# Output projection opened inside the attention of a two-layer streaming trunk: six tiles over the finished heads as fill, and the last memory head from PSUM into the projection's operand

## The chip, the cores and the metric

The kernel runs on one core of one Trainium2 chip. The metric is the device time of one execution in microseconds (us); the comparison uses the median of several runs. A profile of one execution gives the times of single instructions.

## The reference

The reference runs a two-layer encoder trunk over 1056 tokens, 1024 of a new stream and 32 of a running one, with a width of 1024. What matters here, for one layer:

```python
h = rmsnorm(x) @ w_in                       # 1024 wide: token mixer | 4 memory query heads
a = pool_mix(h[:, :512])                    # layer 0; differential attention in layer 1
k, v = split(rmsnorm(mem) @ w_mem)          # 256 memory tokens, 4 heads of 128
m = softmax(q @ k.T * 128 ** -0.5) @ v      # memory attention; the 32 sample tokens use cached k, v
x = x + concat(a, m) @ w_out                # output projection, 1024 x 1024
x = x + relu(rmsnorm(x) @ w1) ** 2 @ w2     # 4096 wide
```

The outputs are `x` after a last norm, the memory keys and values, and pooling and key/value caches.

## The kernel before

Activations lie transposed, features on the 128 partitions: 8 chunks `c` of 128 features. The 1056 tokens are three groups `g` of 352 columns (`GW`). All products are made in full fp32 precision from two parts: a high part (a cast by ScalarE) and a low part (a subtraction on VectorE or on GpSimd, which the profile calls POOL), see `split`. A product is three matmuls (`mm3`): high by high, low by high, high by low. So in the trace lines L49, L50 and L51 are all matmuls of that kind, L54 and L55 the split.

A program run has four stages: start and mixing of layer 0 (`mix0`), output projection and feed-forward of layer 0 (`tail(0)`), mixing of layer 1 (`mix1`), `tail(1)`. Each stage has its own PSUM pool (`ps0` to `ps3`).

In the mixing stages a driver (`drive`, `step`) runs the steps of the attention units (a head's scores, its softmax, and later its transposes and values) and takes steps of a generator `fill0` or `fill1` between them, so that TensorE has other products to do while a softmax runs. The memory attention goes over four heads of two halves of 512 tokens; the 32 sample tokens of all four heads are one further unit, `mem_sample`. `mem_values` transposes the probabilities (L391), splits them (`aTh`, `aTl`), multiplies by the values, copies the result from PSUM (`mo`) and stores it to the DRAM scratch `oscr[l][4 + h]`; the token mixer's heads go to `oscr[l][0..3]`.

`tail(l)` loads the 24 tiles `o` (one for each group and chunk, 176 KB) from `oscr`, splits them into `xh[g]`, `xl[g]` (`take`; for chunks 1, 3 and 5 POOL makes the low part), and loads `x`. `project` then multiplies by `w_out`, a row of weights `W[j]` for each output chunk `j`. Before any other tile it opens six (`g` 0 and 1 by `j` 0 to 2) over chunks 0 to 6, in PSUM banks `xb` and `dn`, and closes them with chunk 7, the last memory head.

Weights stream from DRAM through a ring of six buffers `wraw` (256 KB each, `NRAW`), and `part` casts and subtracts them into `whi`, `wlo` (eight buffers each, `NW`); `weights` lists their order and the engine that subtracts. All these loads, and all stores, are issued by one queue, SP, in program order; an issue that must wait holds those behind it. Within an engine the order of the instructions is set by a scheduler when the program is built, from the order in the code; the engine then takes them strictly in that order. Tile names in the listings below carry a number; `pr` are probabilities, `st` softmax sums, `mk` and `mv` the memory keys and values in parts, `mkr` and `mvr` as loaded, `mks` and `mvs` as just projected, `ms` the sample's, `dh` and `dl` the parts of the pooled difference, `S` its running sums.

Of the kernel before, what the change touches and what calls it, by code (L numbers as in the profile page):

```python
# [17 lines left out]
NS = 32  # L18
# [22 lines left out]
class Kern:  # L41
# [15 lines left out]
    def weights(self):  # L57

        t, v, g = self.t, self.nc.vector, self.nc.gpsimd
        for k in (0, 1, 2, 3):  # L60
            yield t["w_in"][k], None, v
        for j in range(8):
            yield t["w_mem"][j], None, v
        yield t["w_in"][4], None, g
        yield t["w_in"][5], None, g
        for j in range(4):
            yield t["w_mem"][8 + j], None, v
        yield t["w_in"][6], None, g
        yield t["w_in"][7], None, g
        for j in range(4, 8):  # L70
            yield t["w_mem"][8 + j], None, v
        for l in range(2):
            if l:
                for h in range(4):
                    yield t["w_kv"][h], GKV, g
                    yield t["w_kv"][4 + h], GKV, g
                    yield t["w_in"][8 + h], GA + 8, g
                for h in range(4):
                    yield t["w_in"][12 + h], GA + 8, g
            for j in (*range(8), 0, 1, 2):  # L80
                yield t["w_out"][8 * l + j], None, v
            yield None
# [66 lines left out]
    def xtile(self):  # L149
        return self.psum.tile([128, 512], F32, tag="xb", name="xb", bufs=4)  # L150

    def banks(self, name, xbanks):

        self.xbanks = xbanks
        return self.tc.tile_pool(name=name, bufs=1, space=bass.MemoryType.PSUM, reuse_waits="tile")

    def mmtile(self):
        return self.psum.tile([128, 512], F32, tag="mm", name="mm", bufs=2)
# [224 lines left out]
    def mem_values(self, l, h, half, p, kv, pr):  # L383
        nc = self.nc
        v = kv[1]
        parts = []
        for a in range(2):
            pt = self.mmtile()
            for i in range(4):
                b = 256 * i + 128 * a  # L390
                nc.tensor.transpose(pt[:, 128 * i:128 * i + 128], pr[:, b:b + 128], self.ident)  # L391
            ph = p.tile([128, 512], F32R, tag="aTh", name="aTh", bufs=2)
            pl = p.tile([128, 512], F32R, tag="aTl", name="aTl", bufs=2)
            self.split(ph, pl, pt)
            parts.append((ph, pl))
            yield 0.6
        po = self.mmtile()
        for a in range(2):
            self.mm3(po, v[:, 0, a], v[:, 1, a], parts[a][0], parts[a][1], a == 0, a == 1)
            yield 0.65  # L400
        o = p.tile([128, 512], F32, tag="os", name="mo", bufs=2)
        nc.scalar.copy(o, po)
        nc.sync.dma_start(self.oscr[l][4 + h][:, 512 * half:512 * half + 512], o)

    def mem_sample(self, l, p, qs):

        nc, t = self.nc, self.t
        kc = self.qp.tile([128, 4, 256], F32, tag="q", name="mkc", bufs=self.nq)
        vc = self.qp.tile([128, 4, 2, 128], F32, tag="q", name="mvc", bufs=self.nq)
        nc.scalar.dma_start(kc, t["cmk"][l])  # L410
        nc.scalar.dma_start(vc, t["cmv"][l])
        yield from self.wait(3)
        sc = self.stile()
        for h in range(4):
            nc.tensor.matmul(sc[NS * h:NS * h + NS, :256], lhsT=qs[:, h, :], rhs=kc[:, h, :], start=True, stop=True)
        pr, rs = self.softmax(p, sc, 128, 1, 256, SC_MEM)
        nc.gpsimd.tensor_scalar(pr, pr, rs[:, 0:1], 1.0, ALU.mult, ALU.mult)
        yield from self.wait(4)
        pt = self.mmtile()[:, :256]
        for a in range(2):  # L420
            nc.tensor.transpose(pt[:, 128 * a:128 * a + 128], pr[:, 128 * a:128 * a + 128], self.ident)
        aT = p.tile([128, 256], F32, tag="aTh", name="msT", bufs=2)
        nc.scalar.copy(aT, pt)
        yield from self.wait(2)
        po = self.mmtile()[:, :128]
        for h in range(4):
            for a in range(2):
                b = 128 * a + NS * h
                nc.tensor.matmul(po[:, NS * h:NS * h + NS], lhsT=vc[:, h, a, :], rhs=aT[:, b:b + NS],
                                 start=a == 0, stop=a == 1)  # L430
        o = p.tile([128, 4, NS], F32, tag="os", name="oss", bufs=2)
        nc.scalar.copy(o.rearrange("p a b -> p (a b)"), po)
        for h in range(4):
            nc.sync.dma_start(self.oscr[l][4 + h][:, SEQ:], o[:, h, :])
        yield 0.6

    def mem_unit(self, l, p, fill, qq, sample):
        for h in range(4):
            self.need(fill, qq, h)
            with self.tc.issue_after(self.last_exp.ins) if self.last_exp else ExitStack():  # L440
                kv = self.mem_load_kv(l, h, p)
            self.last_exp = None
            if h == 3:
                self.side.append(sample)
            for half in range(2):
                yield from self.backlog(2)
                yield from self.mem_scores(p, kv, qq[h][half], ("m", l, h, half))
                self.later(3, self.mem_values(l, h, half, p, kv, self.mem_pr))
# [187 lines left out]
    def fill0(self, p, mp, dd, qq, qs, U):  # L636
# [17 lines left out]
            yield from self.mem_kv(1, j, mp)  # L654
        yield from self.mem_project(0, 2, p, qq, qs)
        yield from self.mem_project(0, 3, p, qq, qs, [("m", 0, 0, 1)])
        for j in range(4, 8):
            yield from self.mem_kv(1, j, mp)
        self.tick()


    def diff_project(self, h, p, out, smp):
# [236 lines left out]
    def mix1(self):  # L899
        self.nq, self.nmk = 4, 1  # L900
        with self.tc.tile_pool(name="attd", bufs=1, reuse_waits="tile") as self.pd, \
# [12 lines left out]
            qs = p.tile([128, 4, NS], F32, name="mqs")  # L914
            fill = self.fill1(p, dd, qq, smp, qs)
            self.drive([self.diff_unit(p, fill, dd, smp), self.mem_unit(1, p, fill, qq, self.mem_sample(1, p, qs))], fill, 0.8)

    def fill1(self, p, dd, qq, smp, qs):
        for h in range(4):
            yield from self.diff_project(h, p, dd, smp)  # L920
        gates = [[("s", 3, 1)], [("s", 3, 3)], [("m", 1, 0, 1)], [("m", 1, 1, 1)]]
        for h in range(4):
            yield from self.mem_project(1, h, p, qq, qs, gates[h])


    def tail(self, l):
        nc, t = self.nc, self.t
        xin = t["xT"] if l == 0 else self.xscr
        with self.tc.tile_pool(name=f"s{l}", bufs=1, reuse_waits="tile") as sp, \
                self.tc.tile_pool(name=f"ff{l}", bufs=1, reuse_waits="tile") as p:  # L930
            o = [sp.tile([128, C, GW], F32, tag=f"s{g}", name=f"o{g}") for g in range(NG)]
            for cs in (range(7), range(7, 8)):
                for g in range(NG):
                    for c in cs:
                        nc.sync.dma_start(o[g][:, c, :], self.oscr[l][c][:, g * GW:(g + 1) * GW])
            for g in range(NG):
                self.alloc_x(g)
                for c in range(C):
                    self.take(o[g][:, c, :], g, c)
            x = [p.tile([128, C, GW], F32, name=f"x{g}") for g in range(NG)]  # L940
            acc = [self.sum_tile(p, g) for g in range(NG)]
            self.claim(p, (("sq", GW, 2),))
# [15 lines left out]
    def bank(self):  # L958

        self.turn += 1  # L960
        if self.turn < 8:
            return (self.xtile if self.turn < 4 else self.dntile if self.turn < 6 else self.mmtile)()[:, :GW]
        return (self.dntile, self.dntile, self.mmtile, self.mmtile)[self.turn % 4]()[:, :GW]

    def project(self, l, sp, p, po, x, acc):
        nc = self.nc
# [4 lines left out]
            self.sumsq_add(acc[g], x[g][:, j, :], j == first[g], p, eng=nc.gpsimd if g < 1 else None)  # L971

        first = (0, 0, 3)
        W = {j: self.weight() for j in range(3)}
        open_ = [(g, j, self.bank()) for g in range(2) for j in range(3)]
        for cs in (range(7), range(7, 8)):
            for g, j, ps in open_:
                for _ in self.g_dense(ps, W[j], g, cs):
                    pass
                if cs[-1] == 7:  # L980
                    added(g, j, ps)
        self.ahead = 0
        for j in range(3, 8):
            self.wdest = (po, 2) if j == 7 else (self.wpool, NW)
# [504 lines left out]
    def run(self):  # L1489
        self.setup()  # L1490
        self.nq, self.nmk = 6, 1
        with self.tc.tile_pool(name="mem", bufs=1, reuse_waits="tile") as mp:
            self.claim(mp, (("wph", 512, 1), ("wpl", 512, 1), ("memx", 2048, 1), ("mh", 2048, 1), ("ml", 2048, 1),
                            ("mr", 256, 1), ("mks", 256, 2), ("mvs", 256, 2)))
            with self.tc.tile_pool(name="mq0", bufs=1, reuse_waits="tile") as self.qp:
                U = [self.pool_tile(g) for g in range(2)]
                with self.banks("ps0", False) as self.psum:
                    self.start(U)
                    self.mix0(U, mp)
        with self.banks("ps1", True) as self.psum:  # L1500
            self.tail(0)
        with self.banks("ps2", False) as self.psum:
            self.mix1()
        with self.banks("ps3", True) as self.psum:
            self.tail(1)


def _tables():
# [75 lines left out]
```

## Time and profile before

| | us |
|---|---|
| median of 3 runs | 2182.49 |
| lowest, highest | 2181.76, 2184.26 |
| profiled execution | 2185.25 |
| its span | 2183.5 |
| TensorE busy in the span | 2126.3 (97%) |
| VectorE, ScalarE, POOL busy | 1675.7, 1127.9, 690.6 |

The span is the time from the first to the last instruction of the profiled execution. Matmul times there overlap: each is given some 0.3 us though they start 0.16 us apart, and busy time counts their union. The granted TensorE clock is 1.00 at full speed and 0.50 at half. A wait is given with the engine and the tile that ended it.

### The profile page before, as it was taken

How to read it: one execution, taken by the hardware profiler on the slowest of the kernel's cores; microseconds unless marked ns; L12 is line 12 of the kernel's file. 1: busy time of each engine (PE TensorE's matmuls, PEld its weight loads, DVE VectorE, ACT ScalarE, POOL GpSimd, SP SyncE). 2: the span in 40 equal slices, each digit the busy share in tenths (PEclk: the TensorE clock that was granted, in tenths of full speed). 3: DMA queues.
4: the chain of work that ended last, by engine and by line, in shares of the span. 5: the costliest groups of instructions: out<-in, count | busy, mean ns of one | idle time of the engine just before them, and what ended most of it. 6: DMA issues, size and time to landing. Idle time of an engine off the chain costs nothing. (4 is left out here: it accounts for less than half of the span.)

```text
span 2183.5 us, 35482 instructions
## 1 busy us (share of the span) xinstructions
PE 2126.3 (97%) x13140; PEld 2080.7 (95%) x13140; DVE 1675.7 (77%) x3013; ACT 1127.9 (52%) x2383; POOL 690.6 (32%) x679
## 2 busy tenths in 40 slices
PE   9999989999999999998999999999999999999997
PEld 8898989999999999998999988999999999999997
DVE  8746488888888888867566776379888888888865
ACT  7446355444444444454566676346444444444455
POOL 1133105324333333335433213103333333343323
PEclk9998999999999999999999999999999999999999
DMA  5536311111111111123222114401111111111112
GB/s 192 185 105 204 116 49 49 54 45 58 39 59 44 54 49 49 54 80 130 77 70 76 57 59 132 159 30 49 58 44 54 46 52 50 48 54 44 59 39 80
DMA packets 92015, 161.19 MB, mean 74 GB/s; under 512 B 13761, under 2 KB 33729, under 8 KB 91329
## 3 DMA queue, kind: packets, MB, share of 16 engines
q1 hardware_dynamic: 90256, 154.66, 22.3%
q10 hardware_dynamic: 1584, 4.26, 0.7%
q8 instruction: 103, 1.69, 0.3%
q14 instruction: 72, 0.58, 0.1%
HBM read 128.80 MB, written 25.88 MB: 71 GB/s over the span
## 5 line engine op out<-in xcount | busy, mean ns | idle before, releaser
L49 PE MATMUL dn<-xh,whi 128*128 128x352 f32 x1216 | 400.7, 330 | 10.0 <-DVE vst L679 3.0
L50 PE MATMUL dn<-xl,whi 128*128 128x352 f32 x1216 | 394.7, 325 | 0.2 <-DVE xl L221 0.2
L51 PE MATMUL dn<-xh,wlo 128*128 128x352 f32 x1216 | 394.8, 325 | 0.0
L103 ACT CAST whi<-wraw 128x512 fp32r<-128x512 f32 x380 | 233.9, 621 | 270.6 <-PE dn L50 140.8
L104 DVE TENSOR_TENSOR wlo<-wraw,whi 128x512 fp32r<-128x512 f32 x340 | 279.5, 826 | 105.5 <-ACT whi L103 104.6
L1293 DVE TENSOR_TENSOR x<-x,mm 128x352 f32<-128x352 f32 x560 | 287.8, 514 | 66.3 <-PE mm L51 66.1
L49 PE MATMUL mm<-h2h,whi 128*128 128x352 f32 x832 | 270.5, 325 | 0.2 <-DVE x L1293 0.2
L51 PE MATMUL mm<-h2h,wlo 128*128 128x352 f32 x832 | 269.0, 323 | 0.0
L50 PE MATMUL mm<-h2l,whi 128*128 128x352 f32 x832 | 267.4, 321 | 0.0
L103 ACT CAST whi<-ws 128x512 fp32r<-128x512 f32 x240 | 148.9, 621 | 229.1 <-PE dn L50 126.2
L49 PEld LDWEIGHTS dn<-xh,whi 128*128 128x128 f32 x1216 | 229.7, 189 | 16.0 <-DVE kst L669 3.3
L1293 DVE TENSOR_TENSOR x<-x,xb 128x352 f32<-128x352 f32 x448 | 223.1, 512 | 27.1 <-PE xb L51 24.0
L50 PEld LDWEIGHTS dn<-xl,whi 128*128 128x128 f32 x1216 | 230.4, 189 | 2.5 <-DVE xl L221 1.0
L51 PEld LDWEIGHTS dn<-xh,wlo 128*128 128x128 f32 x1216 | 230.0, 189 | 0.2
L55 POOL TENSOR_TENSOR h2l<-t,h2h 128x352 fp32r<-128x352 f32 x112 | 137.2, 1225 | 177.2 <-ACT h2h L54 177.2
L104 DVE TENSOR_TENSOR wlo<-ws,whi 128x512 fp32r<-128x512 f32 x240 | 185.6, 775 | 4.2 <-ACT whi L103 4.2
L55 POOL TENSOR_TENSOR h2l<-b,h2h 128x352 fp32r<-128x352 f32 x92 | 116.0, 1274 | 226.3 <-PE mm L51 204.6
L49 PE MATMUL dn<-T,whi 128*128 128x352 f32 x512 | 166.3, 325 | 1.7 <-ACT u L1208 1.7
L51 PE MATMUL dn<-T,wlo 128*128 128x352 f32 x512 | 166.4, 325 | 0.0
L50 PE MATMUL dn<-T,whi 128*128 128x352 f32 x512 | 166.2, 325 | 0.0
L49 PEld LDWEIGHTS mm<-h2h,whi 128*128 128x128 f32 x832 | 156.2, 188 | 0.9 <-DVE x L1293 0.5
L50 PEld LDWEIGHTS mm<-h2l,whi 128*128 128x128 f32 x832 | 156.3, 188 | 0.4
(306 smaller groups left out, 5283.1 us busy)
## 6 DMA issues: line engine op xcount, KB each, us to landing
wraw<-in_w_ff SPq DMA_DIRECT2D x256, 256.0 KB, 2.6
wraw<-in_w_out SPq DMA_DIRECT2D x44, 256.0 KB, 3.0
o<-oscr SPq DMA_DIRECT2D x48, 176.0 KB, 3.3
wraw<-in_w_mem SPq DMA_DIRECT2D x32, 256.0 KB, 3.2
wraw<-in_w_in SPq DMA_DIRECT2D x30, 256.0 KB, 3.1
xscr<-x SPq DMA_DIRECT2D x3, 1408.0 KB, 4.8
out_y<-x SPq DMA_DIRECT2D x24, 176.0 KB, 1.8
oscr<-mo SPq DMA_DIRECT2D x16, 256.0 KB, 2.1
```

Of the source, the lines that this page charges most:

```text
L49: mm(ps, lhsT=ah, rhs=bh, start=first, stop=False, skip_group_check=more)
L50: mm(ps, lhsT=ah, rhs=bl, start=False, stop=False, skip_group_check=more)
L51: self.last_mm = mm(ps, lhsT=al, rhs=bh, start=False, stop=last, skip_group_check=more)
L55: (lo_eng or self.nc.vector).tensor_tensor(lo, src, hi.bitcast(F32), ALU.subtract)
L103: self.nc.scalar.copy(hi, src)
L104: eng.tensor_tensor(lo, src, hi.bitcast(F32), ALU.subtract)
L1293: nc.vector.tensor_tensor(xj, xj, ps, ALU.add)
```

## The change

1. `open_tiles`, called at the end of `fill0` and `fill1`, takes over the six open tiles: it loads and splits chunks 0 to 6 (`head`; chunks 4 to 6, memory heads 0 to 2, after their stores are issued) and multiplies all 126 products of the six tiles over those chunks as steps of the fill generator. Two of the tiles lie in `dn` banks, four in halves of two score tiles, taken after the last head's scores. The loads go into the weight ring `wraw`, and VectorE makes all low parts.
2. The last memory head (chunk 7) and its sample part are split from PSUM, or from the sample's tile, straight into `xh`, `xl`; their copies, stores and loads go.
3. `project` starts with chunk 7 of the six tiles and only then changes the PSUM pool; the weights of output chunks 4 to 7 are now loaded behind `x`.
4. The low parts of four weight rows of `w_in` are made by VectorE in place of POOL.

```diff
@@ weights
-        yield t["w_in"][4], None, g
-        yield t["w_in"][5], None, g
+        yield t["w_in"][4], None, v
+        yield t["w_in"][5], None, v
...
-        yield t["w_in"][6], None, g
-        yield t["w_in"][7], None, g
+        yield t["w_in"][6], None, v
+        yield t["w_in"][7], None, v
@@ mem_values
-        o = p.tile([128, 512], F32, tag="os", name="mo", bufs=2)
-        nc.scalar.copy(o, po)
-        nc.sync.dma_start(self.oscr[l][4 + h][:, 512 * half:512 * half + 512], o)
+        if h < 3:
+            o = p.tile([128, 512], F32, tag="os", name="mo", bufs=2)
+            nc.scalar.copy(o, po)
+            nc.sync.dma_start(self.oscr[l][4 + h][:, 512 * half:512 * half + 512], o)
+            self.done.add(("o", l, h, half))
+            return
+        for g in range(NG):
+            a, b = max(512 * half, g * GW), min(512 * half + 512, (g + 1) * GW)
+            if a < b:
+                s = slice(a - g * GW, b - g * GW)
+                self.split(self.xh[g][:, C - 1, s], self.xl[g][:, C - 1, s], po[:, a - 512 * half:b - 512 * half])
@@ mem_sample
-        for h in range(4):
+        for h in range(3):
             nc.sync.dma_start(self.oscr[l][4 + h][:, SEQ:], o[:, h, :])
+        s = slice(GW - NS, GW)
+        self.split(self.xh[2][:, C - 1, s], self.xl[2][:, C - 1, s], o[:, 3, :])
+        self.done.add(("o", l, "s"))
@@ fill0 (fill1 likewise)
         yield from self.mem_project(0, 3, p, qq, qs, [("m", 0, 0, 1)])
+        self.new_x(0)
         for j in range(4, 8):
             yield from self.mem_kv(1, j, mp)
         self.tick()
+        yield from self.open_tiles(0)
@@ new functions
+    def open_tiles(self, l):
+        W = self.W = {}
+        self.open = []
+        for c in range(C - 1):
+            if c > 3:
+                for key in (("o", l, c - 4, 0), ("o", l, c - 4, 1), ("o", l, "s")):
+                    yield from self.until(key)
+            self.head(l, c)
+            if c < 3:
+                W[c] = self.weight()
+        places = [(0, 0), (0, 1), (0, 2), (1, 0), (1, 1), (1, 2)]
+        for n, (g, j) in enumerate(places):
+            if n == 2:
+                yield from self.until(("m", l, 3, 1))
+                X = [t[:, 512 * i:512 * i + 512] for t in (self.sctile(), self.sctile()) for i in range(2)]
+            ps = (self.dntile() if n < 2 else X[n - 2])[:, :GW]
+            self.open.append((g, j, ps))
+            yield from self.g_dense(ps, W[j], g, range(C - 1))
+
+    def head(self, l, c):
+        for g in range(NG):
+            o = self.wpool.tile([128, 512], F32, tag="wraw", name="o", bufs=NRAW)[:, :GW]
+            self.nc.sync.dma_start(o, self.oscr[l][c][:, g * GW:(g + 1) * GW])
+            self.take(o, g, c, pool=())
@@ project
-        W = {j: self.weight() for j in range(3)}
-        open_ = [(g, j, self.bank()) for g in range(2) for j in range(3)]
-        for cs in (range(7), range(7, 8)):
-            for g, j, ps in open_:
-                for _ in self.g_dense(ps, W[j], g, cs):
-                    pass
-                if cs[-1] == 7:
-                    added(g, j, ps)
+        W = self.W
+        for g, j, ps in self.open:
+            for _ in self.g_dense(ps, W[j], g, range(C - 1, C)):
+                pass
+            added(g, j, ps)
+        self.banks(True)
```

What this does to the order of instructions, at three places.

TensorE in layer 0, from the last head's scores on (`sc`), before. Transposes of the probabilities `pr`, of the sample's, and the values' products follow each other:

```order
L49 MATMUL sc_2454<-mk_2293,mq_1981 128x256
L50 MATMUL sc_2454<-mk_2293,mq_1981 128x256
L51 MATMUL sc_2454<-mk_2293,mq_1981 128x256
L391 MATMUL mm_2499<-ident_158,pr_2418 128x128 x4
L421 MATMUL mm_2508<-ident_158,pr_2448 128x128 x2
L391 MATMUL mm_2513<-ident_158,pr_2418 128x128 x4
L49 MATMUL mm_2522<-aTh_2504,mv_2294 128x512
L50 MATMUL mm_2522<-aTl_2505,mv_2294 128x512
L51 MATMUL mm_2522<-aTh_2504,mv_2294 128x512
L49 MATMUL mm_2522<-aTh_2518,mv_2294 128x512
L429 MATMUL mm_2526<-msT_2511,mvc_2315 128x32 x8
```

The same place now; `dn_2668` and `dn_2693` are the first two open tiles:

```order
L49 MATMUL sc_2544<-mk_2299,mq_1981 128x256
L50 MATMUL sc_2544<-mk_2299,mq_1981 128x256
L51 MATMUL sc_2544<-mk_2299,mq_1981 128x256
L395 MATMUL mm_2589<-ident_158,pr_2508 128x128 x4
L50 MATMUL dn_2668<-xl0_2157,whi_2362 128x352
L434 MATMUL mm_2598<-ident_158,pr_2538 128x128 x2
L51 MATMUL dn_2668<-xh0_2156,wlo_2363 128x352
L49 MATMUL dn_2693<-xh0_2156,whi_2430 128x352
L50 MATMUL dn_2693<-xl0_2157,whi_2430 128x352
L51 MATMUL dn_2693<-xh0_2156,wlo_2431 128x352
L395 MATMUL mm_2603<-ident_158,pr_2508 128x128 x4
```

Products of the open tiles now stand between the transposes, and likewise behind the steps before and after these rows; 12 of them stand ahead of the values' product of the half before.

SP in layer 1, around the load of the last head's keys (`mkr`), before: loads `o` of groups and chunks, then the keys:

```order
L935 DMA o2_15591<-oscr10_95 128x352
L935 DMA o2_15591<-oscr11_96 128x352
L935 DMA o2_15591<-oscr12_97 128x352
L935 DMA o2_15591<-oscr13_98 128x352
L935 DMA o0_15589<-oscr15_100 128x352
L356 DMA mkr_15376<-kscr13_78 128x256
L403 DMA oscr15_100<-mo_15344 128x512
L935 DMA o1_15590<-oscr15_100 128x352
L361 DMA mvr_15382<-vscr13_86 128x256
L403 DMA oscr16_101<-mo_15432 128x512
```

The same place now:

```order
L978 DMA o_15423<-oscr11_96 128x352
L978 DMA o_15427<-oscr11_96 128x352
L86 DMA wraw_15431<-in_w_out 128x512
L408 DMA oscr15_100<-mo_15357 128x512
L86 DMA wraw_15433<-in_w_out 128x512
L360 DMA mkr_15479<-kscr13_78 128x256
L978 DMA o_15443<-oscr12_97 128x352
L978 DMA o_15447<-oscr12_97 128x352
L978 DMA o_15451<-oscr12_97 128x352
L86 DMA wraw_15455<-in_w_out 128x512
```

Loads `o` and the weight tiles of `w_out` now alternate in the ring of six buffers, ahead of the keys and right behind them. ScalarE's order around the cast of those keys (`mk`), before:

```order
L54 CAST aTh_15352<-mm_15347 128x512
L530 ACTIVATE pr_15332,st_15331<-sc_15277,st_15331 128x256 x4
L54 CAST mq_15152<-qf_15371 128x320
L54 CAST mk_15378<-mkr_15376 128x256
L54 CAST aTh_15395<-mm_15390 128x512
L411 DMA mvc_15400<-in_cmv 128x1024
L54 CAST xh0_15616<-o0_15589 128x352
```

and now:

```order
L54 CAST aTh_15365<-mm_15360 128x512
L547 ACTIVATE pr_15345,st_15344<-sc_15290,st_15344 128x256 x4
L54 CAST mq_15165<-qf_15384 128x320
L54 CAST xh2_15393<-o_15403 128x352
L54 CAST xh2_15393<-o_15427 128x352
L103 CAST whi_15435<-wraw_15431 128x512
L103 CAST whi_15439<-wraw_15433 128x512
L54 CAST xh0_15389<-o_15443 128x352
L54 CAST xh1_15391<-o_15447 128x352
L54 CAST mk_15481<-mkr_15479 128x256
L54 CAST aTh_15498<-mm_15493 128x512
```

The cast of the keys has moved behind casts of `o` tiles and of a weight row.

TensorE in layer 0 at the last pooled row, before. The first products of the pooled difference (`dh`) stand behind one memory head's projection (`dn_1154`) and its transposes, and the next head's projection behind them:

```order
L49 MATMUL dn_1154<-mh_688,whi_1083 128x256
L50 MATMUL dn_1154<-ml_689,whi_1083 128x256
L51 MATMUL dn_1154<-mh_688,wlo_1084 128x256
L326 MATMUL dn_1187<-ident_158,mks_1119 128x128 x2
L49 MATMUL mm_1368<-dh_1234,wph_515 128x352
L50 MATMUL mm_1368<-dl_1235,wph_515 128x352
L51 MATMUL mm_1368<-dh_1234,wpl_516 128x352
L49 MATMUL mm_1389<-dh_1234,wph_515 128x352
L49 MATMUL dn_1208<-mh_688,whi_1146 128x256
```

Now:

```order
L49 MATMUL dn_1208<-mh_688,whi_1150 128x256
L50 MATMUL dn_1208<-ml_689,whi_1150 128x256
L51 MATMUL dn_1208<-mh_688,wlo_1151 128x256
L330 MATMUL dn_1246<-ident_158,mks_1194 128x128 x2
L49 MATMUL mm_1368<-dh_1234,wph_515 128x352
L50 MATMUL mm_1368<-dl_1235,wph_515 128x352
L51 MATMUL mm_1368<-dh_1234,wpl_516 128x352
L49 MATMUL mm_1389<-dh_1234,wph_515 128x352
L49 MATMUL dn_1271<-xh0_172,whi_1200 128x352
```

The 24 products of the next head (`dn_1208`) and its transposes have moved ahead of the pooled row.

More of the change, by code (lines that the diff above doesn't have):

```diff
@@ L150, in xtile, with banks @@
         return self.psum.tile([128, 512], F32, tag="xb", name="xb", bufs=4)
-    def banks(self, name, xbanks):
+    def banks(self, xbanks):
+        if self.psum_pool:
+            self.psum_pool.__exit__(None, None, None)
+        self.n_pools += 1
         self.xbanks = xbanks
-        return self.tc.tile_pool(name=name, bufs=1, space=bass.MemoryType.PSUM, reuse_waits="tile")
+        self.psum_pool = self.tc.tile_pool(name=f"ps{self.n_pools}", bufs=1, space=bass.MemoryType.PSUM, reuse_waits="tile")
+        self.psum = self.psum_pool.__enter__()
     def mmtile(self):
@@ L413, in mem_sample @@
         sc = self.stile()
+        self.done.add(("m", l, "s"))
         for h in range(4):
@@ L443, in mem_unit @@
             if h == 3:
+                self.need(fill, self.done, ("x", l))
                 self.side.append(sample)
@@ L916, in mix1 @@
             self.drive([self.diff_unit(p, fill, dd, smp), self.mem_unit(1, p, fill, qq, self.mem_sample(1, p, qs))], fill, 0.8)
+            for w in fill:
+                assert w is not None
     def fill1(self, p, dd, qq, smp, qs):
@@ L923, in fill1, with new_x @@
             yield from self.mem_project(1, h, p, qq, qs, gates[h])
+        self.new_x(1)
+        yield from self.open_tiles(1)
+    def new_x(self, l):
+        for g in range(NG):
+            self.alloc_x(g)
+        self.done.add(("x", l))
+    def open_tiles(self, l):
[17 more added lines that the diff above has]
+    def head(self, l, c):
+        for g in range(NG):
+            o = self.wpool.tile([128, 512], F32, tag="wraw", name="o", bufs=NRAW)[:, :GW]
+            self.nc.sync.dma_start(o, self.oscr[l][c][:, g * GW:(g + 1) * GW])
+            self.take(o, g, c, pool=())
     def tail(self, l):
@@ L930, in tail @@
                 self.tc.tile_pool(name=f"ff{l}", bufs=1, reuse_waits="tile") as p:
-            o = [sp.tile([128, C, GW], F32, tag=f"s{g}", name=f"o{g}") for g in range(NG)]
-            for cs in (range(7), range(7, 8)):
[L933 to L939, printed above, removed]
+            self.claim(sp, tuple((f"s{g}", C * GW, 1) for g in range(NG)))
             x = [p.tile([128, C, GW], F32, name=f"x{g}") for g in range(NG)]
@@ L960, in bank @@
         self.turn += 1
-        if self.turn < 8:
-            return (self.xtile if self.turn < 4 else self.dntile if self.turn < 6 else self.mmtile)()[:, :GW]
-        return (self.dntile, self.dntile, self.mmtile, self.mmtile)[self.turn % 4]()[:, :GW]
+        return (self.mmtile, self.mmtile, self.dntile, self.dntile)[self.turn % 4]()[:, :GW]
     def project(self, l, sp, p, po, x, acc):
@@ L973, in project @@
         first = (0, 0, 3)
-        W = {j: self.weight() for j in range(3)}
-        open_ = [(g, j, self.bank()) for g in range(2) for j in range(3)]
-        for cs in (range(7), range(7, 8)):
-            for g, j, ps in open_:
-                for _ in self.g_dense(ps, W[j], g, cs):
-                    pass
-                if cs[-1] == 7:
-                    added(g, j, ps)
+        W = self.W
[4 more added lines that the diff above has]
+        self.banks(True)
         self.ahead = 0
@@ L1491, in run @@
         self.nq, self.nmk = 6, 1
+        self.psum_pool, self.n_pools = None, 0
+        self.banks(False)
         with self.tc.tile_pool(name="mem", bufs=1, reuse_waits="tile") as mp:
@@ L1496, in run @@
                 U = [self.pool_tile(g) for g in range(2)]
[L1497 to L1505, printed above, removed]
+                self.start(U)
+                self.mix0(U, mp)
+        self.tail(0)
+        self.banks(False)
+        self.mix1()
+        self.tail(1)
+        self.psum_pool.__exit__(None, None, None)
 def _tables():
```

## The prediction

> **What bounds the kernel now.** I read the page's busy table and slices first, then stretches of the span, then TensorE's waits in the bad stretches, and last the instructions at their edges. The engine table:
>
> ```profile
> span 2183.5 us, 35482 instructions
> PE 2126.3 (97%) x13140; PEld 2080.7 (95%) x13140; DVE 1675.7 (77%) x3013; ACT 1127.9 (52%) x2383; POOL 690.6 (32%) x679
> ```
>
> TensorE is the bound and lacks only 57 us (2183.5 - 2126.3). No change that leaves the matmuls as they are can win more than those idle 57 us and what TensorE loses in stretches of low granted clock. By stretch (TensorE's busy time stands after the comma, its granted clock after POOL's):
>
> ```profile
> core 0: us, PE busy (x) PEld busy (x) DVE busy (x) ACT busy (x) POOL busy (x), PEclk, DMA share, GB/s
> 50.00:110.00 60.00, 54.90 (x372) 53.03 (x373) 46.89 (x80) 28.58 (x62) 10.82 (x7) 0.97 0.57 176
> 190.00:216.00 26.00, 21.59 (x101) 16.96 (x100) 17.73 (x31) 18.36 (x51) 12.24 (x14) 0.74 0.73 230
> 216.00:300.00 84.00, 84.00 (x527) 83.57 (x526) 46.23 (x83) 30.21 (x55) 6.63 (x7) 1.00 0.29 101
> 1330.00:1380.00 50.00, 43.30 (x239) 36.57 (x238) 32.31 (x63) 31.96 (x93) 18.31 (x25) 0.89 0.48 147
> ```
>
> The projection (from 216 on) runs full and fast. The attention's end ahead of it does not: 190 to 216 and 1330 to 1380 are where the last memory head of each layer is alone on TensorE. The waits there, first layer 0, then layer 1 (us in total, times, longest):
>
> ```profile
> PE mm L49 <- ACT aTh L54: 2.1, 1, 2.1
> PE mm L49 <- DVE aTl L55: 0.8, 2, 0.5
> ...
> PE sc L49 <- ACT pr L530: 1.5, 1, 1.5
> PE mm L49 <- ACT aTh L54: 1.3, 1, 1.3
> ```
>
> They are links of one chain (scores, softmax, transposes, split, values) with no other matmul to run meanwhile. The edges: the last head's transposes of layer 0, the first open matmul, the point where the clock has come back, and the end of the six open tiles; then the same of layer 1 without the clock's.
>
> ```profile
> 190.26 0.60 PE L391 MATMUL mm<-ident,pr 128*128 128x128 f32 x4
> ...
> 212.15 0.49 PE L49 MATMUL xb<-xh,whi 128*128 128x352 f32 x1
> ...
> 214.72 0.32 PE L49 MATMUL xb<-xh,whi 128*128 128x352 f32 x1
> ...
> 236.33 0.32 PE L49 MATMUL mm<-xh,whi 128*128 128x352 f32 x1
> ...
> 1349.64 0.60 PE L391 MATMUL mm<-ident,pr 128*128 128x128 f32 x4
> ...
> 1376.52 0.49 PE L49 MATMUL xb<-xh,whi 128*128 128x352 f32 x1
> ...
> 1400.36 0.33 PE L49 MATMUL mm<-xh,whi 128*128 128x352 f32 x1
> ```
>
> From 214.72 to 236.33 stand the last 135 of the 144 open matmuls: 0.160 us each. Before 214.72 they come every 0.29 (nine in 2.57 us): half clock.
>
> **The open tiles as fill, layer 0.** The change takes 126 of the 144 matmuls (chunks 0 to 6: 6 x 7 x 3), 126 x 0.160 = 20.2 us of work, and lets TensorE do them between the links of the chain. It removes no matmul. What can be won is what is lost there now: idle 26.00 - 21.59 = 4.4 us, and by the clock 26 x (1 - 0.74) = 6.8 us, together 11.2.
>
> What it adds to the chain: the six-buffer weight ring now carries the loads of the finished heads, and their casts and subtractions stand in the rows of ScalarE and VectorE ahead of softmax steps.
>
> ```profile
> L935 SPq DMA_DIRECT2D o<-oscr x48: 320/430/664, 192.2 to 1379.8; - x48
> L54 ACT CAST xh<-o x48: 476/488/579, 195.8 to 1383.3; 128x352 fp32r<-128x352 f32 x48
> L55 DVE TENSOR_TENSOR xl<-o,xh x30: 510/526/1264, 198.1 to 1383.8; 128x352 fp32r<-128x352 f32 x30
> L55 POOL TENSOR_TENSOR xl<-o,xh x18: 926/941/1306, 196.9 to 1378.2; 128x352 fp32r<-128x352 f32 x18
> ...
> DMA to landing us min/median/max: 2.2/3.3/4.3
> ...
> oscr<-oss SPq DMA_DIRECT2D x4, 16.0 KB, 1.5
> ```
>
> Nine subtractions of each layer go from POOL to VectorE: 9 x 0.526 = 4.7 us more VectorE work, in a stretch where it is busy 17.73 of 26. The three of chunk 3 (1.6 us) and their casts stand ahead of the last head's first softmax half: I put that chain 2 us later. Against it the 12 open matmuls that the new order sets ahead of the values' matmuls cover 1.9 us of a chain that waited 2.9 already (2.1 + 0.8), and more stand behind each next link. I leave 0.9 us idle there. Following the order at these prices, 56 of the 126 are done when the last values' matmul ends (about 209.8). Chunks 0 to 4 have 90, so 34 are left for 5.4 us, until 215.2. Chunk 5's first load stands on SP behind the three small stores of the sample heads (ready about 208.5: three issues at 0.43, 1.5 us to land, 211.3), then one load's issue, 3.3 us to land, 0.49 cast, 0.53 subtraction: 216.1 to 216.3. So about 1.1 us idle. Sum: 11.2 - 0.9 - 1.1 = 9.2 by the stretch. Followed through the order instead, the other 70 open matmuls and chunk 7's 18 (14.1 us) end near 226 in place of 236.33, 10.3. I take **9.5**, nearer the stretch's, since its idle and clock are read and not followed by hand. Range 3 (half clock stays, and one more stall) to 12.
>
> The clock is what this hangs on. It fell at waits this short:
>
> ```profile
> 200.00:205.00 5.00, 3.31 (x13) 2.81 (x14) 4.38 (x8) 3.04 (x10) 3.20 (x4) 0.60 0.93 324
> 205.00:210.00 5.00, 4.48 (x17) 3.49 (x17) 1.38 (x4) 3.18 (x8) 0.94 (x2) 0.50 0.28 71
> ```
>
> After 1.7 us idle out of 5, with no wait over 2.1 us, the clock stood at half for the next 5 us although TensorE was busy 4.48. With idle pieces of 0.9 and 1.1 us, ten microseconds apart, I expect full clock in layer 0. The Trainium skill ("TensorE: Matmul & The Clock Gate", Part 1) has the clock halve after at least one idle window of about 3.4 us. By that rule neither the 2.1 us wait before nor any stall named here would halve it, and the clock's 6.8 us would not have been lost at all; this trace halves it after less, so the sum does not use it; by it the 0.8 us set aside for layer 1's clock below would fall away (2162).
>
> **Layer 1.** Cap: idle 50.00 - 43.30 = 6.7, clock 50 x 0.11 = 5.5, together 12.2. Here the last head's keys suffer. Their load stands on SP behind four loads of finished heads and four weight tiles, in a ring of six; and their cast on ScalarE stands behind two weight casts and two chunk-2 casts, whose loads are issued after the keys' own.
>
> ```profile
> 1347.44 0.32 SPq L356 DMA_DIRECT2D mkr<-kscr  x1
> ...
> 1351.01 0.42 ACT L54 CAST mk<-mkr 128x256 fp32r<-128x256 f32 x1
> ```
>
> I put that load at 1349.2, the chunk-2 loads behind it as buffers of the ring come free and 3.3 us to land, and the cast at 1355.9 in place of 1351.01: the chain starts some 5 us late. The fill covers part; three stalls stay (1.4 at the scores, 1.6 at the softmax, 1.2 at the second half) and 2.0 us at chunk 5, since two of chunk 4's loads and the sample's stores come later than in layer 0: 6.2 us. The six tiles then end at about 1393.2 in place of 1400.36, 7.2 us. Stalls of 1.4 to 2 us are of the size that halved the clock above; one half-clock window costs 1.7 us (in steps of 3.4 us, half of each), at even odds 0.8. I take **6.4**; by the stretch alone 12.2 - 6.2 = 6.0. Range -3 (the chain late by the cap and more) to 12.
>
> **Weight rows from POOL to VectorE, 78 to 95.** The four low parts that POOL made in one stretch:
>
> ```profile
> 78.31 0.68 DVE L104 TENSOR_TENSOR wlo<-wraw,whi 128x512 fp32r<-128x512 f32 x1
> 78.90 1.28 DVE L574 TENSOR_TENSOR S<-U 128x1085 f32<-128x1085 f32 x1
> 80.22 2.27 DVE L574 TENSOR_TENSOR S<-S 128x1083 f32<-128x1083 f32 x1
> ...
> 82.75 4.29 DVE L574 TENSOR_TENSOR S<-S 128x1079 f32<-128x1079 f32 x2
> ...
> 79.39 8.80 POOL L104 TENSOR_TENSOR wlo<-wraw,whi 128x512 fp32r<-128x512 f32 x4 [29.59 <-ACT whi L103]
> ...
> PE mm L49 <- ACT dh L54: 3.1, 2, 2.6
> PE dn L326 <- DVE mks L315: 1.3, 1, 1.3
> ...
> 188.00 0.28 PE L50 MATMUL dn<-ml,whi 128*128 128x256 f32 x1
> 188.12 0.28 PE L51 MATMUL dn<-mh,wlo 128*128 128x256 f32 x1
> ```
>
> The same add took 1.28 us when it began ahead of POOL's 8.80 us and about 2.2 under it. Without POOL, three adds lose 0.9 us each, 2.7, and the four subtractions give VectorE 4 x 0.68 = 2.7 back: VectorE itself is as late as before, and the gain must come from the order. There, 24 matmuls of a memory head's projection (128x256, 0.12 us from one start to the next, 2.9 us) and two transposes now stand ahead of the pooled row's first matmul, whose wait was 2.6 us: it goes. The 1.3 us wait for `mks` goes if the adds are shorter, since `mks` stood between two long ones. 2.6 + 1.3 and little of the clock: **4.0**. Bounds: idle 60.00 - 54.90 = 5.1 plus clock 60 x 0.03 = 1.8 above, 6.9; below 0, if the adds stay at 2.2 and the new subtractions push the row 2.7 us back into the cover. I take the middle, nearer the top because the 2.6 us wait is covered either way.
>
> **The rest.** The last head leaves PSUM straight into its parts: two copies, two stores, one small store and three loads of each layer go, six pairs of pieces come on ScalarE and VectorE. They stand at the end of the chain, ahead of chunk 7 only, which comes 70 matmuls (11 us) later: nothing. Between 165 and 190 ScalarE and VectorE take the first chunks' parts (0.49 and 0.53 us each) in a stretch where TensorE hardly waits; a cast that comes ahead of an exponential delays it by its own 0.49, and where the tiles behind it cover that is open: **-0.5**, between 0 and -3 (six of them). Weight row 4 now loads after the six big loads of `x`:
>
> ```profile
> x<-in_xT SPq DMA_DIRECT2D x3, 880.0 KB, 10.8
> x<-in_xT SPq DMA_DIRECT2D x3, 528.0 KB, 6.6
> ```
>
> Behind the six tiles (226.0) one tile of row 3 runs (24 x 0.16 = 3.8), then row 4 is needed, at about 229.9. With `x` issued as its tiles come free, near 215 to 219, and the last of it landing 10.8 us later, the row's parts are ready at about 229.2. Nothing, with 0.7 us to spare; without it each microsecond costs one per layer.
>
> Sum: 9.5 + 6.4 + 4.0 - 0.5 = 19.4 us. Against the profiled execution (2185.25 us, span 2183.5) that is 2165.9; it was 2.8 us above the median of the runs, so against 2182.49 **2163**.
>
> **Rivals.**
> - *All of it lands.* No stall outlasts the fill, and the clock stays full: 11.2 + 12.2 + 6.9 = 30.3, 2152. For it: 20 us of fill against chains that wait under 3 us. Against: the chunk-5 loads depend on the sample's store.
> - *The clock stays half.* Stalls of about 2 us in each last head suffice, as at 200. Then the 6.8 and 5.5 us are not won, only the idle and the first place: about 19.4 - 9, 2172. The same comes out if row 4 is late by 4 us a layer.
> - *The ring starves the chain* (the other side). Loads, weight rows and the last head's keys share six buffers and one issue queue; ScalarE takes its casts in row, so one late load holds a softmax. If each of four turns of the ring per layer takes 6.6 us, as the 528 KB loads did, in place of 3.3, a chain is 13 us later: 26 - 19.4, slower by 7, 2189. It decides from some 10 us per layer on. Against it: such loads never took over 4.3 us.
> - *Nothing to see.* The parts cancel: layer 1 loses what layer 0 gains, within 4 us.
>
> **How the numbers follow.** A measurement of this kernel tells about 0.2%, 4.4 us. The forecast (14 to 25 us won) 0.50; all of it (beyond 25) 0.12; half clock or late row (4.4 to 14) 0.24; nothing 0.07; slower 0.07. Faster 0.86. The range takes in the caps (2152, and 2 us for idle that a modelled matmul end hides) and reaches up to where a loss of layer 1's and a half clock leave 5 us; it leaves out the last two: 2150 to 2177.
>
> **What would show it.** In layer 0: `xh,whi` matmuls between the transposes from 190 on, granted clock 1.0 in 200 to 214, row 3's first matmul near 226. In layer 1: the last key cast near 1356 less the 13 us won before, stalls on `sc` and `aTh`, the six tiles closing 7 us sooner after their first transposes than now. Near 90, no 2.6 us wait. I am wrong if the clock column stays at 0.5 after 200, if `wraw` or `o` is what ScalarE waits for through the last softmax, or if `wlo` of row 4 holds TensorE in the projection.

## The result: 16.8 us faster, and where they came from

The changed kernel took 2166.55 us (median of 4 runs, 2164.87 to 2167.28) against 2183.38 for the kernel before (4 runs, one of them 2190.12): ratio 0.9916, 95% interval 0.9894 to 0.9938. (The ratio weighs all runs, the 2190.12 too; the medians alone give 0.9923.) The profiled execution took 2165.92 us, 19.3 less than the profiled execution before (2185.25); the forecast for it was 2165.9, and 2163 for the median.

The page after, first lines:

```profile
span 2164.1 us, 35480 instructions
PE 2116.5 (98%) x13140; PEld 2073.5 (96%) x13140; DVE 1680.3 (78%) x3043; ACT 1126.8 (52%) x2383; POOL 658.9 (30%) x653
```

The same 13140 matmuls; idle time fell from 57 to 48 us, less than the span did. Most of the rest is the granted clock, which the stretches show (TensorE's busy time after the comma, its clock third from the end):

```profile
core 0: us, PE busy (x) PEld busy (x) DVE busy (x) ACT busy (x) POOL busy (x), PEclk, DMA share, GB/s
50.00:110.00 60.00, 57.29 (x394) 55.89 (x393) 45.76 (x85) 29.14 (x62) 3.46 (x5) 0.97 0.59 182
190.00:216.00 26.00, 25.89 (x164) 23.78 (x163) 14.90 (x35) 13.87 (x41) 2.94 (x5) 1.00 0.49 165
1330.00:1380.00 50.00, 44.69 (x273) 38.75 (x272) 31.90 (x65) 27.79 (x76) 7.70 (x13) 1.00 0.62 209
```

From 190 to 216 TensorE is idle for 0.1 us in place of 4.4, at a clock of 1.00 in place of 0.74: 164 matmuls run there, 101 before. In layer 1 it is idle for 5.3 us in place of 6.7, at 1.00 in place of 0.89; the changed kernel is some 13 us ahead there, so these two stretches hold partly different work. The edges after, in the order of those before (last transposes ahead of the open tiles, first open matmul, first matmul of weight row 3; then row 3 in layer 1):

```profile
186.92 0.60 PE L395 MATMUL mm<-ident,pr 128*128 128x128 f32 x4
...
188.02 0.43 PE L49 MATMUL dn<-xh,whi 128*128 128x352 f32 x1
...
223.16 0.43 PE L49 MATMUL mm<-xh,whi 128*128 128x352 f32 x1
...
1382.23 0.32 PE L49 MATMUL mm<-xh,whi 128*128 128x352 f32 x1
```

Row 3 of layer 0 starts 13.2 us sooner (236.33 to 223.16), of which 3.3 were won ahead of the last head (190.26 to 186.92). In layer 1 it starts 18.1 us sooner (1400.36 to 1382.23). To split a run by place, I compare the start of the matmul of the same number, counted from 0, in both traces (times are the kernel before's), from the 450th (79 us) to the 600th (108 us) for the pooled row's place, the 1150th to the 1450th (186 to 243 us) for layer 0 and the 8150th to the 8600th (1340 to 1425 us) for layer 1. The order changes inside a place and agrees at its ends.

| us against the kernel before | forecast | changed kernel | again, other execution |
|---|---|---|---|
| pooled row | -4.0 | -2.4 | -1.4 |
| end of layer 0's attention | -9.5 | -9.9 | -9.1 |
| end of layer 1's attention | -6.4 | -5.2 | -2.5 |
| all else | +0.5 | -1.8 | -2.6 |

"All else" is what is left of the difference between the profiled executions (19.4 forecast, 19.3 and 15.6 measured). The last column is the run named e12_after below. In layer 1 the clock differs there: in that execution it fell to half once more in this place, for 6.8 us. The two executions of one kernel thus differ by 0.8 to 2.7 us a place, and single profiles are read with that scatter in mind; the kernel before scatters likewise, from 2179 to 2188 us beside the experiments, with the mean clock from 0.989 to 0.984.

### The profile page after: what moved, and what is told of

The parts are those of the page before. It is cut to its first block, busy times and chain, and to the rows that moved or that the text cites. A ratio compares the mean times of both kernels' runs of the same rounds, so it can differ in the third digit from the quotient of the medians.

```text
span 2164.1 us, 35480 instructions
## 1 busy us (share of the span) xinstructions
PE 2116.5 (98%) x13140; PEld 2073.5 (96%) x13140; DVE 1680.3 (78%) x3043; ACT 1126.8 (52%) x2383; POOL 658.9 (30%) x653
## 5 line engine op out<-in xcount | busy, mean ns | idle before, releaser
L104 DVE TENSOR_TENSOR wlo<-wraw,whi 128x512 fp32r<-128x512 f32 x348 | 285.9, 827 | 81.1 <-ACT whi L103 80.4
```

The costliest lines, as they stand in the source:

```text
L104: eng.tensor_tensor(lo, src, hi.bitcast(F32), ALU.subtract)
```

## Experiments

All times are medians; ratios are to the kernel before, measured beside each run on the same chip (2184.83 us beside e1 to e4, 2183.86 beside e5, e6, e7 and e9, 2186.5 beside e10 to e13). They weigh all runs and so differ a little from the quotient of the medians. The 95% interval stands in brackets. "By place" is the profiled execution against the kernel before's, as in the table above.

**e12_after.** The changed kernel, again.

> The changed kernel once more, beside the three below on one chip: 0.9915 to 0.9925 of the kernel before, 2165 to 2168 us.

2169.66 us, 0.9918 [0.9904, 0.9931]: the ratio as expected, the absolute time 1.7 us above the range; the kernel before was also slower beside it (2186.5 against 2183.38).

**e13_loads_only.** Loads and splits stay inside; the products go behind the last head.

```diff
 open_tiles:
-            yield from self.g_dense(ps, W[j], g, range(C - 1))
+            yield 0.45
 project:
+        for g, j, ps in self.open:
+            steps = self.g_dense(ps, W[j], g, range(C - 1))
+            with self.tc.issue_after(self.last_mm.ins):
+                next(steps)
+            for _ in steps: pass
```

> The changed kernel with the loads and splits of the finished heads inside the attention as they are, but all 126 products of the open tiles behind the last head's last value product. Theory A (the gain is products of the open tiles standing between the steps of the last head): without them the chain stands bare again, and later by what the loads push it back, the clock falls: no better than part 4 alone, 0.998 to 1.003. Rival N (it is the early loads and parts that gain, the products may stay behind): 0.995 or less.

2191.48 us, 1.0026 [1.0017, 1.0036]: slower than before, as theory A had it, and rival N is out. By place: pooled row -2.2, layer 0 +2.6, layer 1 +6.1. TensorE's waits from 186 to 245 us, then from 1325 to 1400:

```profile
PE mm L49 <- DVE aTl L55: 1.7, 1, 1.7
PE mm L395 <- DVE aTl L55: 1.4, 1, 1.4
...
PE sc L49 <- ACT mk L54: 3.3, 1, 3.3
PE mm L49 <- DVE aTl L55: 2.3, 2, 1.2
```

This is the chain without its fill, and the clock falls again (to half for 3.4 us at 191 and 10.2 us at 201). The cast of the last head's keys, which the forecast put 5 us late in layer 1, is late (3.3 us of wait on `mk`); in the changed kernel the open tiles' products cover it wholly.

**e4_two_tiles.** Two open tiles inside (42 matmuls), four behind.

```diff
-        places = [(0, 0), (0, 1), (0, 2), (1, 0), (1, 1), (1, 2)]
+        places = [(0, 0), (0, 1)]
 project, behind self.banks(True):
+        for g, j in [(0, 2), (1, 0), (1, 1), (1, 2)]:
+            ps = self.bank()
+            self.dense(ps, W[j], g)
+            added(g, j, ps)
```

> The changed kernel with two open tiles inside the attention in place of six (42 matmuls, 6.7 us of fill); the other four run behind, all chunks at once. Theory A (the gain is the covered chain, and in the changed kernel the steps after the last softmax are covered by the third to sixth tile): those steps, about 8 us long with 3.5 us of fill in them, stand bare again, the clock falls there: 3 to 5 us lost in layer 0 and 2 to 4 in layer 1, 0.994 to 0.9955. Rival D (any small fill keeps the clock full, and the clock is most of the gain): within 1.5 us of the changed kernel, 0.9916 to 0.9923.

2181.18 us, 0.9988 [0.9979, 0.9996]. Rival D is out, and theory A gave too little: layer 0 keeps 4.7 of 9.9 us, near what A had; layer 1 goes from 5.2 won to 4.2 lost, 9.4 us where A allowed 2 to 4. Its stretch from 1335 to 1400:

```profile
1335.00:1400.00 65.00, 56.18 (x305) 48.47 (x306) 39.53 (x79) 33.75 (x89) 8.74 (x13) 0.89 0.62 211
```

8.8 us idle and the clock at 0.89, where the changed kernel has 5.4 and 1.00 in the same stretch: with this little fill, the lateness that loads and casts bring into layer 1 is no longer covered. A third of the fill brings a seventh of the gain (0.12% of 0.84%).

**e7_dummy.** The kernel before with useless matmuls in the chain of layer 0.

```diff
 mem_values, behind self.split(ph, pl, pt); tr is the last transpose:
+            if l == 0 and h == 3:
+                ps = self.dntile()[:, :GW]
+                with self.tc.issue_after(tr.ins):
+                    for k in range(8):
+                        nc.tensor.matmul(ps, lhsT=self.wph[:, 0, :], rhs=self.wph.rearrange("p a b -> p (a b)")[:, :GW], start=k == 0, stop=k == 7)
```

> The kernel before with 32 matmuls of 128x352 added whose results nobody reads, eight behind each group of the last head's transposes in layer 0 (5.1 us at full clock). Theory K (the clock is the larger part of layer 0's gain and falls for idle time alone): the half clock of 201 to 214 goes, 6.8 us less, some 2.5 of the added 5.1 us lie in idle time: 4 us faster than the kernel before, 0.998. Rival L (the clock falls for another reason than idle time there): the added work costs 2.5 us and the clock stays at half, 1.001.

2186.19 us, 1.0009 [1.0000, 1.0018]. Neither theory: the clock did come back (stretch 200 to 205 below, 0.60 before), yet layer 0 ended as late as before (-0.2 us, in an execution of 2182.33 us, the fastest of its eleven). The last values' product came 2.9 us sooner (208.86 against 211.73), although 5.1 us of useless work stood in the chain; the 2.9 us then went, 2.0 of them into a new wait for the loaded heads' parts. First a stretch, then the longest of these waits:

```profile
200.00:205.00 5.00, 3.98 (x27) 3.06 (x26) 1.61 (x4) 1.46 (x5) 1.12 (x2) 1.00 0.01 3
...
210.81 0.75 PE L49 MATMUL xb<-xh,whi 128*128 128x352 f32 x3 [1.57 <-ACT xh L54]
```

So getting the clock back this way wins nothing in layer 0, where the open tiles' operands come no sooner, and early loads without fill (e13) lose. The fill here is work that nobody needs; what useful fill without early loads would win, this run does not show, and the open tiles can't be had without their operands.

**e3_head_dram.** The last head through the scratch, as before (part 2 undone).

```diff
 mem_values, mem_sample: copy and store for every head
 tail:
+            self.head(l, C - 1)
```

> The changed kernel with part 2 undone: the last memory head and its sample go through PSUM copies, stores to the scratch and three loads again, now through the weight ring. Theory A: the 70 matmuls of the open tiles that are left when the last value product ends (11 us) cover copy, store, load and split (0.6 + 2.1 + 3.3 + 1.0 and some issues, 8 us): 0 to 1 us slower than the changed kernel, 0.9916 to 0.9921. Rival C (chunk 7 then waits on the ring and the issue queue, behind the loads of chunks 4 to 6): 3 to 6 us slower a layer, 0.994 to 0.997.

2176.92 us, 0.9963 [0.9950, 0.9976]: 10 us lost, theory A wrong. The size is rival C's, its reason is not. TensorE's waits from 205 to 245 us:

```profile
PE mm L49 <- ACT whi L103: 1.7, 1, 1.7
PE dn L49 <- ACT xh L54: 0.5, 1, 0.5
PE mm L51 <- DVE wlo L104: 0.5, 1, 0.5
```

Chunk 7 itself is hardly waited for (0.5). What is late is weight row 4: its loads stand behind `x`, and `x` now stands behind the last head's store and loads. SP's first issues of the weights behind `x` in the changed kernel, and of `x` and the weights here:

```profile
211.30 20.62 SPq L86 DMA_DIRECT2D wraw<-in_w_out  x14
...
214.19 1.33 SPq L990 DMA_DIRECT2D x<-in_xT  x3
215.57 2.38 SPq L992 DMA_DIRECT2D x<-in_xT  x3
218.05 20.10 SPq L86 DMA_DIRECT2D wraw<-in_w_out  x14
```

The weights are 6.8 us later, and TensorE waits 2.2 us for them in each layer (1.7 and 0.5 above, 1.8 and 0.4 in layer 1). Layer 0 keeps 6.3 us, layer 1 nothing (+0.6, with one more stretch of half clock at 1394); the waits for the weights are thus about half of the loss by place.

**e9_dram_ring.** The same, with the loads of chunks 0 to 6 in four buffers of their own.

```diff
 head, for c < 7:
-            o = self.wpool.tile([128, 512], F32, tag="wraw", name="o", bufs=NRAW)[:, :GW]
+            o = self.hp.tile([128, GW], F32, tag="ohd", name="o", bufs=4)
```

> The last memory head through the scratch again (part 2 undone), with the loads of chunks 0 to 6 in four buffers of their own. Theory M (undoing part 2 cost 8 to 10 us because three more loads in the shared ring pushed x and weight row 4 behind the point where TensorE needs it): half of that or more comes back, 4 to 7 us faster than with part 2 undone alone. Rival C (chunk 7's own way through the scratch is what TensorE waits for): no faster than that by over 1.5 us.

2169.36 us, 0.9930 [0.9917, 0.9942]: 7.2 us come back by the ratios, theory M. Layer 0 is at -9.1, layer 1 at -5.3, and TensorE waits for no weight where e3 waited. SP's issues in layer 0:

```profile
212.01 1.38 SPq L86 DMA_DIRECT2D wraw<-in_w_out  x3
213.50 1.55 SPq L990 DMA_DIRECT2D x<-in_xT  x3
```

The first of these weights now go ahead of `x`, which itself leaves hardly sooner than in e3. So part 2's worth is in the main not a shorter way for the last head: it keeps row 4 early. How much of that is the ring and how much the queue stays open, since this run takes all 21 loads of chunks 0 to 6 out of the ring, and not three.

**e6_own_ring_p4.** The changed kernel with those four buffers.

> The changed kernel with the loads of finished heads in four buffers of their own, so that weights keep the ring of six to themselves; weight row 4 then loads ahead of x. Theory G (layer 1 loses its 3 us of waits for casts of loaded heads to the shared ring): 2 to 3 us faster than the changed kernel, all in layer 1. Rival H (those waits come from the loads' own landing time and ScalarE's order): within 0.8 us of it.

2168.15 us, 0.9924 [0.9911, 0.9938]: no gain (the changed kernel has 0.9916 and 0.9918), so theory G is not borne out and H is left. From 1325 to 1400 TensorE waits for loaded heads as long as without the new buffers (first line; the changed kernel's own follow):

```profile
PE dn L49 <- ACT xh L54: 2.9, 4, 1.3
...
PE dn L49 <- ACT xh L54: 3.0, 4, 1.3
PE mm L49 <- DVE aTl L55: 1.1, 1, 1.1
PE mm L395 <- ACT mo L407: 0.7, 1, 0.7
```

**e1_weights_pool, e2_weights_only.** Part 4 undone, and part 4 alone (`g` for `v` in four lines of `weights`, and the reverse).

> The changed kernel with part 4 undone: POOL again makes the low parts of the four weight rows. Theory A (the parts add up; this one is worth what the traces differ by between 83 and 100 us, 2.4 us): about 2.4 us slower than the changed kernel, near 0.9930 of the kernel before, with the running sums back at 2.2 us each, and the layers' ends unchanged (row 3 of layer 0 starts 10 us, not 13, sooner than before). Rival B (the place's gain comes from the open tiles' loads and order, not from the weights): no slower than the changed kernel, 0.9916.

> The kernel before with part 4 alone. Theory A: the pooled row's place gains 2.4 us and nothing else changes, 0.9989 of the kernel before. The forecast's working gave this part 4.0 us, 0.9982. Rival B: within 0.5 us of the kernel before, 1.000.

2170.73 us, 0.9940 [0.9928, 0.9952], and 2183.02 us, 0.9995 [0.9987, 1.0004]. In the place itself e1 has -1.2 and e2 -1.5 us, where the changed kernel has -2.4 and -1.4, and e7, which changes nothing there, has -1.2: part 4 can't be told from the scatter of single profiles. The traces show why: the wait moves. TensorE's waits from 60 to 110 us in e2:

```profile
PE dn L49 <- ACT mvs L328: 3.5, 1, 3.5
PE dn L49 <- DVE mks L315: 1.8, 1, 1.8
```

In that stretch the runs without part 4 (the kernel before, e1, e7) wait 4.5 to 4.7 us in all, mostly for `mks` and `dh`; those with it wait 2.7 (changed kernel), 4.2 (e12) and 5.3 us (e2), mostly for `mvs`. Alone part 4 gains at most 2.8 us in the median (lower end of e2's interval), so the forecast's 4.0 is out. Undoing it cost more in the median (4.8 us by the ratios of e1 and e12, whose intervals overlap slightly); the part of this beyond the place was not resolved.

**e10_os3.** Three buffers for outgoing copies in place of two (`bufs=3` for the tag `os`).

> The changed kernel with three buffers in place of two for the copies that go out to the scratch. At 88 us TensorE waits 2.5 us for a copy of memory values that stands on ScalarE behind a pooled copy, which waits 1.0 us for its buffer's store to land. Theory P (that store is the cause): 1 to 2 us faster than the changed kernel of this call. Rival Q (the copy then waits as long for weight casts or the pooled sums): within 0.5 us of it.

2167.51 us, 0.9912 [0.9898, 0.9925]. In the place, -4.9 us against -1.4 for the changed kernel beside it (e12). TensorE's waits from 60 to 110 us, of e12_after (two rows) and then of this run:

```profile
PE dn L49 <- ACT mvs L332: 3.4, 1, 3.4
PE dn L49 <- DVE mks L319: 0.8, 1, 0.8
...
PE dn L49 <- ACT mvs L332: 0.9, 1, 0.9
PE dn L49 <- DVE mks L319: 0.5, 1, 0.5
```

The trace bears out theory P, with more than its size in the place (3.5 us), since the half clock there went too. By the ratios it is 1.3 us, within the intervals, so the time does not decide.

**e5_close_then_add.** All six closings, then all six adds.

```diff
             for _ in self.g_dense(ps, W[j], g, range(C - 1, C)):
                 pass
+        for g, j, ps in self.open:
             added(g, j, ps)
```

> The changed kernel with the six closings in one row and the six adds behind them. In the changed kernel two closings wait for an add to another half of the same pair of banks (0.4 us each at the weights' load, 0.8 us in layer 0 and 0.5 in layer 1). Theory F (these waits are tied to the pair of banks, not to the half): both go, 1.0 to 1.3 us faster than the changed kernel. Rival: the first matmul of weight row 3 waits for the last adds in their place, no difference.

2165.61 us, 0.9913 [0.9900, 0.9927], against 0.9916 for the changed kernel: not told apart by time. In the trace one of two waits is gone. The changed kernel's weight loads from 216 to 236 us had

```profile
PEld sc L49 <- DVE x L1015: 0.4, 1, 0.4
PEld mm L49 <- DVE x L1015: 0.4, 1, 0.4
```

The first, at a closing (221.80), is not there in this run; the second, at the first matmul of weight row 3, stays at 0.4 (layer 0 -10.4 us). So theory F holds for the closing alone, and the second wait was never one of the closings'.

**e11_best.** Both.

> Three buffers for outgoing copies, and the six closings in one row with the adds behind them. By the sum of the two (1 to 2 us and about 1.2 us): 2 to 3 us faster than the changed kernel of this call, 0.990 to 0.991 of the kernel before. If the waits only move: within 0.7 us of the changed kernel.

2164.2 us, 0.9904 [0.9891, 0.9918]: 3.1 us below the changed kernel (e12) by the ratios, near the 2 to 3 of the sum, and the lowest median here; the intervals overlap. By place -4.9, -9.6 and -5.6.

## Why the forecast held, point by point

- **Layer 0: right in size, partly by luck.** The cap of 11.2 us was the right frame, and 9.9 were won where 9.5 were put down. The 2.0 us of stalls did not come: chunk 5 is never waited for, and the only wait of TensorE from 160 to 216 us is

```profile
PE mm L395 <- ACT mo L407: 0.3, 1, 0.3
```

  In their place 0.8 us went behind the open products, 0.4 at a closing and 0.4 at the first product of row 3, both waiting for an add that the working had not seen; e5 removes the first. That the clock stays full held in both profiled executions of the changed kernel. The working read the fall of the clock from the stretch 200 to 205, but it falls at 201.0: ahead of it TensorE was idle 2.0 of 3.4 us (197.46 to 200.87, last section), not 1.7 of 5.
- **Layer 1: mechanism right, the stalls elsewhere.** The cast of the last keys is late, and in the changed kernel starts at

```profile
1341.26 0.42 ACT L54 CAST mk<-mkr 128x256 fp32r<-128x256 f32 x1
```

  against 1351.01 before, 9.8 us sooner where TensorE had got 12.9 us ahead (matmul 8150): 3.1 us late, not 4.9. The 1.4 us put down for it at the scores are covered (e13 shows them bare). TensorE waits 3.0 us for the open tiles' own parts, since in its fixed order it meets products whose loads have just landed or not yet (at 1347 ScalarE itself waits 1.6 us for one), 1.1 us for `aTl` and 0.7 for `mo`. 5.2 us won against 6.4. The half clock set down at even odds for one 3.4 us window came in one of two executions, for two windows.
- **The pooled row: the step that failed** is that the 2.6 us wait "goes" and is won. The pooled sums did run at 1.28 us, and from 60 to 110 us TensorE no longer waits for `dh`. But it now waits as long at the first of the 24 products that were to cover that wait, for the copy of the memory values. The changed kernel's waits there, and the copies on ScalarE:

```profile
PE dn L49 <- ACT mvs L332: 2.5, 1, 2.5
PE dn L49 <- DVE mks L319: 0.2, 1, 0.2
...
86.80 0.55 ACT L620 ACTIVATE po<-mm,gains 128x352 f32<-128x352 f32 x1 [1.02 <-DMA oscr<-po]
...
87.76 0.37 ACT L332 COPY mvs<-dn 128x256 f32<-128x256 f32 x1
```

  ScalarE's row, in order: a pooled copy waits for a store to land, a weight cast follows, then `mvs`. With part 4 alone the same wait is there (e2, 3.5 us), and with one more buffer for outgoing copies it falls to 0.9 (e10). The working asked which matmuls cover the old wait, and not what the covering matmuls themselves wait for. 1.4 to 2.4 us won against 4.0.
- **The last head from PSUM: priced at nothing, worth about 10 us.** The step weighed only the copies and stores taken away and the cover behind them. It costed row 4 with 0.7 us to spare, and did not ask how much of that margin this part supplied: without it row 4 is issued 6.8 us later (e3), and with row 4 issued early again most of the loss comes back (e9). The forecast had named a late row 4 as a way to lose 4 us a layer, but tied it to `x` alone.
- **The rivals.** "The ring starves the chain" did not happen with six tiles. e4 and e13 show a chain made late when there is less fill; that the ring makes it late is not shown, and in the changed kernel four buffers of its own win nothing (e6). "All of it lands" comes near in layer 0 only (9.9 of 11.2). "The clock stays half" was wrong for layer 0. "Nothing to see" is out, with the interval's upper end at 0.9938.
- **The total** hit within 4 us for the median and to the tenth for the profiled execution; with terms off by 1 to 2 us of both signs and clock windows of 1.7 us each coming and going, the tenth is chance.

## What to carry to other kernels

Fill wins only with its operands there: moving products into a chain's gaps and moving their loads ahead are one change. Here the loads alone lost (e13), and useless products in layer 0's gaps, which brought the clock back, gained nothing (e7). When a wait is covered by other work, list what that work waits for on each engine and queue; here it waited for a copy behind a store, and one more buffer took most of that wait away in the trace (e10). A part that looks like tidying (one head's trip through memory) may be what lets the loads of the next stage leave in time.

## What the runs showed of the hardware

The granted clock of TensorE fell behind stretches that were only partly idle, and not at the same places in two executions of one program. Stretches of the kernel before, ahead of two falls, then of e12_after, ahead of a half clock and in it:

```profile
197.46:200.87 3.41, 1.40 (x7) 0.90 (x7) 2.90 (x7) 3.41 (x13) 1.72 (x2) 1.00 0.94 282
1323.85:1327.26 3.41, 3.41 (x25) 3.12 (x24) 1.19 (x2) 0.00 (x0) 0.03 (x1) 1.00 0.27 77
...
1346.60:1350.10 3.50, 1.33 (x8) 0.75 (x6) 3.42 (x6) 2.29 (x6) 0.00 (x0) 0.96 0.74 247
1350.10:1356.90 6.80, 6.65 (x23) 5.72 (x24) 4.28 (x12) 4.21 (x15) 1.82 (x3) 0.52 0.12 44
```

In e12_after TensorE was busy 1.33 of 3.50 us, so the stretch was not idle as a whole, and then ran at half speed for 6.8 us although busy nearly throughout. In the profiled execution of the same kernel told above, no half clock came between 1330 and 1380, at the same kind of waits. The granted clock changes in steps of 3.41 us in every trace here, and ahead of most falls stands a 3.4 us stretch with 0 to 2.1 us of busy time. One fall in each trace, between 1310 and 1330, comes behind a stretch in which TensorE was busy throughout (second row); no run here shows why. The Trainium skill ("TensorE: Matmul & The Clock Gate", Part 1) has windows of that length, free-running, which agrees, and an idle window as the condition, which is stricter than what these rows show. For a reader of such numbers it means that a kernel with gaps of one to two microseconds can vary by some microseconds between executions by the clock: 6.8 us at half clock are 3.4 us lost, and the two executions of the changed kernel differ by 2.7 us in layer 1's place.
